# One layer of a hybrid attention / gated-linear-attention encoder: the product of probabilities and V in plain float32, two heads side by side in the column halves of the TensorE array

## The chip, the core and the metric

The kernel runs on one core of a Trainium2 chip. The metric is the device time of one execution in microseconds (us). Inputs and output are float32.

## What is computed

One layer: a LayerNorm of `x` (2048 frames x 1024), one input projection, two groups of heads, an output projection, a gated embedding and a second LayerNorm. The change lies in group A, chunked softmax attention with 8 heads of 64. Cut to what matters:

```python
h = layer_norm(x, ln_in_g, ln_in_b)
proj = h @ w_in                       # aq, ak, av, ag (512 each), then group B's parts
# per 64-frame chunk c and head: its own chunk and the 8 chunks before it
sc = einsum('bhqd,bhkd->bhqk', q_blk, k_blk) * scale + bias
sc = where(valid, sc, -1e30)
pr = softmax(sc, axis=-1)
att = einsum('bhqk,bhkd->bhqd', pr, v_blk)       # the product that is changed
att = att * silu(ag)
mix = concatenate([att, gla * silu(gg)]) @ w_out
```

Group B is gated linear attention with 4 heads. It is not touched, but some of its products have the form that the change brings in.

## The kernel before

The 2048 frames are two super-blocks `sb` of 1024, and each of these two groups `g` of 512 frames. For each super-block three phases follow each other: `gla_phase` (group B), `attn_phase` (group A) and `out_phase` (output projection, embedding, LayerNorm).

**Precision by halves.** The kernel gives most products to the array in a type `F32R`, rounded, which shows as one matmul record in the trace for each matmul of the program. To keep float32's accuracy it splits an operand into a rounded copy (`hi`) and the rest (`lo`) and adds the products: three matmuls (`hi*hi`, `hi*lo`, `lo*hi`) make one product of the projections (`gemm`, L317; V's own projection `gemm_v`, L917). A product of two plain `F32` operands shows as two records for each matmul.

**Attention.** `attn_phase` works on four pairs `pr` of heads. Each step of `attn` is one block of 128 queries of one head `h`: `pr`, `g`, then `h`, `qp` (which pair of query blocks) and `a` (which block of the pair). For a step
- `S` makes the scores, up to 5 key blocks of 128, with Q in halves (L993, L995); DVE adds the bias and takes the maximum (L999), ACT takes the exponential and the sum (L1003), and `norm` divides on POOL (L1011);
- `T` turns the probabilities block by block on TensorE (L1029, three blocks to a PSUM tile `PT`, of which there are two), and takes them out of PSUM twice: ACT writes the rounded copy `PTh` (L1031), DVE the rest `PTl` (L1032);
- `PV`, once for each head and pair of query blocks (64 calls), multiplies by V. Its weights are the 128 columns [hi of V | lo of V] of one head and key block, and its moving operand is 256 queries of `PTh`, then of `PTl`: 12 matmuls for a full call of 6 key blocks, each 128 columns wide (L1049). The first and the last of a call's key blocks concern only 128 of the queries. So the 128 partitions of the result `PV` hold 64 rows of products with V's hi and 64 with its lo;
- `fold`, for each head and group (32 times), adds these two: ACT copies one half of the partitions (L1062), DVE adds the other (L1063). After the second head DVE multiplies by the SiLU gate (L1065).

`ev_v` splits V into hi and lo as it leaves PSUM (ACT L932, DVE L933) and stores to DRAM (`vhist`) what a later step needs; `v_load` and `hist` fetch it.

**What sets the order.** Attention's steps run beside the projections as a side generator: `gemm` calls `tick()` every 4 matmuls, and the generator is advanced by as much as its due times say. The framework's scheduler then orders each engine's queue.

Of the kernel before, what the change touches and what calls it, by code (L numbers as in the profile page):

```python
# [26 lines left out]
F32 = mybir.dt.float32  # L27
F32R = mybir.dt.float32r
I32 = mybir.dt.int32
AF = mybir.ActivationFunctionType  # L30
OP = mybir.AluOpType
# [13 lines left out]
def hymba_layer_kernel(  # L45
# [15 lines left out]
    nc = tc.nc  # L61
    seq = x.shape[0]
    NSB = seq // 1024
# [6 lines left out]
    pool_t = ctx.enter_context(tc.tile_pool(name="pool_t", bufs=4))  # L70
    small = ctx.enter_context(tc.tile_pool(name="small", bufs=4))
    dram = ctx.enter_context(tc.tile_pool(name="dram", bufs=1, space=bass.MemoryType.DRAM))
# [3 lines left out]
    def U(name, dt=F32):  # L76
        return pool_u.tile([128, 512], dt, name=name, tag="u")
# [50 lines left out]
    mix = [[None, None] for _ in range(8)]  # L128
# [356 lines left out]
    def silu_evac(ps, k, g, first):  # L485
        t = U("t")
        nc.scalar.activation(t, ps, AF.Tanh, scale=0.5)
        if first:
            mix[k][g] = U("mix")
            nc.vector.scalar_tensor_tensor(mix[k][g], t, 1.0, ps, op0=OP.add, op1=OP.mult)  # L490
        else:
            nc.vector.scalar_tensor_tensor(t, t, 1.0, ps, op0=OP.add, op1=OP.mult)
            nc.vector.scalar_tensor_tensor(mix[k][g], t, 0.5, mix[k][g], op0=OP.mult, op1=OP.mult)
# [1 line left out]

    Fd = dram.tile([8, 64, 768], F32, name="relrows")
    khist = dram.tile([4, 2, 128, 512], F32, name="khist")
    vhist = dram.tile([2, 4, 2, 2, 128, 512], F32, name="vhist")

    def rel_load():  # L500
        ext = pool_t.tile([128, 6, 256], F32, name="ext", tag="t").rearrange("p a b -> p (a b)")[0:8, 0:768]
# [368 lines left out]
    def attn_phase(sb):  # L870
        es = ExitStack()
        aps = None
        Q = {}
        K = {}
        V = {}
# [49 lines left out]
                w_done(i + 1)  # L925

        def ev_v(ps, pr, g, bp):
            p5 = ps.rearrange("p (b e h d) -> p b e h d", b=2, e=2, h=2)
            for e in range(2):
                t = U("v", F32R)  # L930
                t4 = t.rearrange("p (b h d) -> p b h d", b=2, h=2)
                nc.scalar.activation(t4[:, :, :, 0:64], p5[:, :, e], AF.Copy)  # L932
                nc.vector.tensor_tensor(t4[:, :, :, 64:128], p5[:, :, e],  # L933
                                        t4[:, :, :, 0:64].bitcast(F32), op=OP.subtract)
                if e == 0:
                    V[pr, g, bp] = t
                if e or g and sb + 1 < NSB:
                    nc.sync.dma_start(vhist[sb % 2, pr + e, g, bp], t.bitcast(F32))

        def v_load(pr, g, bp):  # L940
            V[pr, g, bp] = t = U("v", F32R)
            nc.sync.dma_start(t.bitcast(F32), vhist[(sb if g >= 0 else sb - 1) % 2, pr, g % 2, bp])

        def hist(pr, h):
            if sb == 0:
                return
            K[pr, -1, h] = t = U("k", F32R)
            nc.sync.dma_start(t.bitcast(F32), khist[pr, h])
            v_load(pr, -1, h)

        bias = {}

        def load_bias(pr, h):
            f = Fd[:]
            bias[pr, h] = t = pool_p.tile([128, 640], F32, name="bias", tag="p")
            nc.gpsimd.memset(t[64:128, 0:64], NEG)
            nc.gpsimd.memset(t[0:64, 576:640], NEG)
            with tc.issue_after(queued[-1]):
                for r0 in (0, 64):
                    nc.sync.dma_start(t[r0:r0 + 64, r0:r0 + 576], bass.AP(  # L960
                        tensor=f.tensor, offset=f.offset + (2 * pr + h) * 64 * 768 + 127,
                        ap=[[767, 64], [1, 576]]))

        steps = [(pr, g, h, qp, a) for pr in range(4) for g in range(2) for h in range(2)
                 for qp in range(2) for a in range(2)]
        st = {}
        pts = {}
        pvs = {}
        att = {}

        def blk(n):
            pr, g, h, qp, a = steps[n]
            i = sb * 8 + g * 4 + 2 * qp + a
            return i, min(i, 4) + 1
# [32 lines left out]
        def norm(n):  # L1007
            ncol = blk(n)[1] * 128
            P, s4 = st[n]
            nc.vector.reciprocal(s4[:, 3:4], s4[:, 2:3])  # L1010
            nc.gpsimd.tensor_scalar(P[:, :ncol], P[:, :ncol], s4[:, 3:4], 1.0,  # L1011
                                    op0=OP.mult, op1=OP.mult)

        def T(n):
            a = steps[n][4]
            i, nkb = blk(n)
            P, _ = st.pop(n)
            if a == 0:
                pts[n // 2] = (pool_t.tile([128, 6, 256], F32R, name="PTh", tag="t"),
                               pool_t.tile([128, 6, 256], F32R, name="PTl", tag="t"))  # L1020
            Th, Tl = pts[n // 2]
            k0 = max(0, i - a - 4)
            d = i - nkb + 1 - k0
            cs = slice(a * 128, (a + 1) * 128)
            for b0 in range(0, nkb, 3):
                nb = min(3, nkb - b0)
                ps = aps.tile([128, 3, 128], F32, name="PT", bufs=2)
                for b in range(nb):
                    nc.tensor.transpose(ps[:, b, :], P[:, (b0 + b) * 128:(b0 + b + 1) * 128], ident)  # L1029
                ks = slice(d + b0, d + b0 + nb)  # L1030
                nc.scalar.activation(Th[:, ks, cs], ps[:, :nb, :], AF.Copy)  # L1031
                nc.vector.tensor_tensor(Tl[:, ks, cs], ps[:, :nb, :], Th[:, ks, cs].bitcast(F32),  # L1032
                                        op=OP.subtract)

        def PV(n):
            pr, g, h, qp, _ = steps[n]
            i, _ = blk(n - 1)
            Th, Tl = pts.pop(n // 2)
            if qp == 0:
                pvs[pr, g, h] = aps.tile([128, 512], F32, name="PV")  # L1040
            pv = pvs[pr, g, h]
            k0 = max(0, i - 4)
            ks = [i] + [b for b in range(k0, i + 2) if b != i]
            jobs = [(T_, b) for T_ in (Th, Tl) for b in ks]
            for m, (T_, b) in enumerate(jobs):
                c0 = 128 if b == i + 1 else 0
                c1 = 128 if b == i - 4 else 256
                gi, kb = b // 4 - 2 * sb, b % 4
                nc.tensor.matmul(pv[:, qp * 256 + c0:qp * 256 + c1],  # L1049
                                 lhsT=V[pr, gi, kb // 2][:, kb % 2 * 256 + h * 128:kb % 2 * 256 + h * 128 + 128],  # L1050
                                 rhs=T_[:, b - k0, c0:c1], start=(m == 0),
                                 stop=(m == len(jobs) - 1))
            if qp == 1:
                fold(pr, g, h)

        def fold(pr, g, h):
            pv = pvs.pop((pr, g, h))
            if h == 0:
                att[pr, g] = U("pvt")
            t = att[pr, g]  # L1060
            r, o = slice(64 * h, 64 * h + 64), slice(64 - 64 * h, 128 - 64 * h)
            nc.scalar.activation(t[r, :], pv[o, :], AF.Copy)  # L1062
            nc.vector.tensor_tensor(t[r, :], pv[r, :], t[r, :], op=OP.add)  # L1063
            if h == 1:
                nc.vector.scalar_tensor_tensor(mix[pr][g], t, 0.5, mix[pr][g],  # L1065
                                               op0=OP.mult, op1=OP.mult)
                del att[pr, g]

        def attn():
            N = len(steps)  # L1070
            for n in range(N + 4):
                if 0 <= n - 1 < N:
                    norm(n - 1)
                if n < N:
                    pr, g, h, qp, a = steps[n]
                    if pr % 2 and n % 8 < 2:
                        v_load(pr, g, n % 8)
                    if g == 1 and qp == 1 and a == 1 and pr < 3:
                        S(n)
                        load_bias(pr + 1, h)  # L1080
                        hist(pr + 1, h)
                    else:
                        S(n)
                yield
                if n >= 4 and steps[n - 4][4] == 1:
                    PV(n - 4)
                if 0 <= n - 2 < N:
                    T(n - 2)
                yield 2

        run = attn()

        def gate(i, pr, g):
            gemm(i, 8, 0, h_rhs(g), lambda ps: silu_evac(ps, pr, g, True), g == 1)

        for pr in range(4):
            odd = pr % 2
            idx = take(4)
            for g in range(2):
# [20 lines left out]
                if aps is None:  # L1120
                    edge.pop("close")()
                    aps = es.enter_context(tc.tile_pool(name="attnps", bufs=1, space=bass.MemoryType.PSUM))
        gg = take(2)
        set_side(run, scale=0.7, delay=1)
        for g in range(2):
            for n in range(2):
                gemm(gg[n], 8, 0, h_rhs(g),
                     lambda ps, n=n, g=g: silu_evac(ps, 6 + n, g, False), g == 1)
# [227 lines left out]
```

## Time and profile before

| | |
|---|---|
| time, three runs | 1384.40, 1390.73, 1391.21 us, median 1390.73 |
| the profiled execution's own time | 1383.77 us |
| its span in the trace | 1381.9 us |
| granted TensorE clock, mean | 0.993 |
| busy: TensorE matmuls, weight loads | 97%, 84% of the span |
| busy: DVE, ACT, POOL | 60%, 44%, 11% |

The profiled execution is 0.5% below the median of the runs and next to the lowest of them. A matmul record's end is modelled, and records overlap each other; how long a run of matmuls really holds the engine is read from the starts: from the first record's start to the start of what follows.

### The profile page before, as it was taken

The page shows a single profiled execution, that of the slowest core. Times are in us where ns is not written, and L with a number is a line of the kernel's source. Part 1 is how long each engine was busy: PE and PEld are TensorE (multiplying, and loading weights), DVE is VectorE, ACT ScalarE, POOL GpSimd, SP SyncE. Part 2 cuts the span into 40 slices and gives each one's busy share as a digit, 9 for nine tenths or more (in the row PEclk, how much of TensorE's full clock was granted, in tenths as well). Part 3 has the DMA queues.
Part 4 walks back from the last instruction along what each step waited for, and adds up shares of the span by engine and source line. Part 5 has one row for each costly group of instructions (what it writes and reads, how often), then busy time and mean ns, then how long its engine had stood idle before and what let it go on. Part 6 is the DMA issues. An engine that isn't in the chain of part 4 may idle for free.

```text
span 1381.9 us, 22143 instructions
## 1 busy us (share of the span) xinstructions
PE 1339.8 (97%) x8440; PEld 1166.5 (84%) x8440; DVE 829.1 (60%) x1833; ACT 609.7 (44%) x1200; POOL 154.0 (11%) x233
## 2 busy tenths in 40 slices
PE   5999999999999999999999999999999999999995
PEld 5889888889888888888898988988998888888875
DVE  7765636766576955546884552566566667332286
ACT  4755525555555722624544542455544555112222
POOL 1000101111111100000100100111211120000012
PEclk9999999999999999999999999999999999999998
DMA  8361516332533335766622132322232213335551
GB/s 323 57 192 48 200 62 229 107 140 71 191 117 130 130 122 197 272 224 229 202 77 108 62 109 80 135 94 90 82 107 101 85 47 111 111 108 196 203 187 61
DMA packets 63441, 186.39 MB, mean 135 GB/s; under 512 B 7216, under 2 KB 9320, under 8 KB 63336
## 3 DMA queue, kind: packets, MB, share of 16 engines
q1 hardware_dynamic: 62816, 183.41, 37.6%
q10 hardware_dynamic: 520, 1.57, 1.1%
q8 instruction: 67, 1.10, 0.3%
q14 instruction: 38, 0.31, 0.1%
HBM read 119.28 MB, written 65.67 MB: 134 GB/s over the span
## 4 chain that ended last, share of the span: by engine, by line
PE 81%; DVE 8%; ACT 5%; issue 2%; DMA 2%; POOL 1%; SPq 0%; ACTq 0%; DVEq 0%; POOLq 0%
PE proj L317 51%; PE proj L917 7%; PE proj L557 4%; PE PV L1049 4%; PE PT L1029 4%; PE S L995 2%; PE S L993 2%; DMA wraw<-in_wi_dram 1%; PE O L704 1%; DVE P L999 1%; ACT P L1003 1%; DVE PTl L1032 1%; ACT whi L286 1%; DVE wlo L291 1%; ACT qh L885 1%
## 5 line engine op out<-in xcount | busy, mean ns | idle before, releaser
L317 PE MATMUL proj<-hh,whi 128*128 128x512 f32 (+1 forms) x912 | 358.8, 393 | 2.3 <-DVE ql L888 0.8
L317 PE MATMUL proj<-hh,wlo 128*128 128x512 f32 (+1 forms) x912 | 357.4, 392 | 0.0
L317 PE MATMUL proj<-hl,whi 128*128 128x512 f32 (+1 forms) x912 | 354.2, 388 | 0.0
L317 PEld LDWEIGHTS proj<-hh,whi 128*128 128x128 f32 x912 | 172.9, 190 | 31.6 <-issue 1.0
L317 PEld LDWEIGHTS proj<-hl,whi 128*128 128x128 f32 x912 | 172.6, 189 | 29.1
L317 PEld LDWEIGHTS proj<-hh,wlo 128*128 128x128 f32 x912 | 172.5, 189 | 29.1
L1003 ACT ACTIVATE P<-P,s 128x640 f32<-128x640 f32 (+4 forms) x128 | 97.5, 762 | 154.7 <-DVE s L1002 134.5
L1011 POOL TENSOR_SCALAR P<-P,s 128x640 f32<-128x640 f32 (+4 forms) x128 | 95.9, 749 | 505.1 <-DVE s L1010 379.4
L999 DVE CUSTOM_DVE_ANT_0 P<-S,bias 128x640 f32<-128x640 f32 (+4 forms) x128 | 94.5, 738 | 48.8 <-PE S L995 42.8
L1032 DVE TENSOR_TENSOR PTl<-PT,PTh 128x384 fp32r<-128x384 f32 (+2 forms) x232 | 102.6, 473 | 14.9 <-ACT PTh L1031 13.1
L317 PE MATMUL proj<-mh,whi 128*128 128x512 f32 x256 | 99.9, 390 | 0.0
L317 PE MATMUL proj<-mh,wlo 128*128 128x512 f32 x256 | 99.8, 390 | 0.0
L159 POOL TENSOR_TENSOR rstd<-v,nhalf 128x1 f32<-128x1 f32 (+2 forms) x44 | 33.2, 761 | 570.9 <-DVE v L157 522.0
L1031 ACT ACTIVATE PTh<-PT 128x384 fp32r<-128x384 f32 (+2 forms) x232 | 87.0, 420 | 20.1 <-PE PT L1029 18.9
L1029 PE MATMUL PT<-ident,P 128*128 128x128 f32 x560 | 84.5, 275 | 1.0 <-DVE PTl L1032 0.8
L291 DVE TENSOR_TENSOR wlo<-wraw,whi 128x1024 fp32r<-128x1024 f32 (+1 forms) x46 | 56.1, 1225 | 46.6 <-ACT whi L286 44.8
L317 PE MATMUL proj<-ml,whi 128*128 128x512 f32 x192 | 75.2, 392 | 0.0
L917 PE MATMUL proj<-whi,hh 128*128 128x256 f32 x256 | 74.5, 291 | 0.0
L557 PE MATMUL proj<-whi,hl 128*128 128x272 f32 (+1 forms) x256 | 74.0, 293 | 0.0
L557 PE MATMUL proj<-whi,hh 128*128 128x272 f32 (+1 forms) x256 | 73.2, 293 | 0.7 <-ACT glr L574 0.7
L917 PE MATMUL proj<-wlo,hh 128*128 128x256 f32 x256 | 72.5, 283 | 0.0
L917 PE MATMUL proj<-whi,hl 128*128 128x256 f32 x256 | 72.4, 283 | 0.0
(221 smaller groups left out, 2512.8 us busy)
## 6 DMA issues: line engine op xcount, KB each, us to landing
whi<-wkept SPq DMA_DIRECT2D x64, 512.0 KB, 3.6
wlo<-wkept SPq DMA_DIRECT2D x64, 512.0 KB, 4.5
wkept<-whi SPq DMA_DIRECT2D x44, 512.0 KB, 2.9
wkept<-wlo SPq DMA_DIRECT2D x44, 512.0 KB, 3.5
wraw<-in_wi_dram SPq DMA_DIRECT2D x26, 512.0 KB, 5.5
x<-in_x_dram SPq DMA_DIRECT2D x32, 256.0 KB, 5.4
out_dram<-ysb SPq DMA_DIRECT2D x32, 256.0 KB, 2.1
v<-vhist SPq DMA_DIRECT2D x24, 256.0 KB, 3.6
```

The source lines that it names most:

```text
L159: nc.gpsimd.tensor_tensor(r[:, :n], v1[:, :n], nhalf[:, :n], op=OP.pow)
L291: nc.vector.tensor_tensor(lo, raw, hi.bitcast(F32), op=OP.subtract)
L317: nc.tensor.matmul(ps[:, cols], lhsT=l[:, c0 + k, :], rhs=rhs(k)[m][:, cols], start=(j == 0), stop=(j == n - 1))
L557: nc.tensor.matmul(ps[:, c0:c0 + nw], lhsT=h[k][g][:, b * 128:(b + 1) * 128], rhs=W[k // 4][m][:, k % 4, :], start=(n == 0), stop=(n == 23))
L917: nc.tensor.matmul(ps[:, bb * 256:bb * 256 + 256], lhsT=h[k][g][:, c], rhs=W[k // 4][m][:, k % 4, :], start=(k == 0 and n == 0), stop=(k = ...
L999: nc.vector.tensor_tensor_reduce(P[:, :ncol], ps[:, 512 - n_prev:512 + n_cur], bias[pr, h][:, 640 - ncol:640], 1.0, -3e38, OP.add, OP.max, ...
L1003: nc.scalar.activation(P[:, :ncol], P[:, :ncol], AF.Exp, bias=s4[:, 1:2], scale=1.0, accum_out=s4[:, 2:3])
L1011: nc.gpsimd.tensor_scalar(P[:, :ncol], P[:, :ncol], s4[:, 3:4], 1.0, op0=OP.mult, op1=OP.mult)
L1029: nc.tensor.transpose(ps[:, b, :], P[:, (b0 + b) * 128:(b0 + b + 1) * 128], ident)
L1031: nc.scalar.activation(Th[:, ks, cs], ps[:, :nb, :], AF.Copy)
L1032: nc.vector.tensor_tensor(Tl[:, ks, cs], ps[:, :nb, :], Th[:, ks, cs].bitcast(F32), op=OP.subtract)
L1049: nc.tensor.matmul(pv[:, qp * 256 + c0:qp * 256 + c1], lhsT=V[pr, gi, kb // 2][:, kb % 2 * 256 + h * 128:kb % 2 * 256 + h * 128 + 128], rh ...
```

## The change

Neither V nor the probabilities are split any more. V is stored once, in float32, for both heads of a pair: a tile of four key blocks by 128 columns, head 0 in columns 0 to 63 and head 1 in 64 to 127. The steps are ordered `qp` before `h`, so the two heads of a pair of query blocks are ready together, and `PV` is called once for both (32 calls). For each key block it issues two float32 matmuls with 64 weight columns each, head 0 into partitions 0 to 63 of the result and head 1 into 64 to 127. The result then holds both heads as the output projection wants them: `fold` is gone, and DVE multiplies by the gate straight from PSUM. `T` takes each `PT` tile out once: the first three blocks by ACT, the others by DVE.

```diff
-    vhist = dram.tile([2, 4, 2, 2, 128, 512], F32, name="vhist")
+    vhist = dram.tile([2, 4, 2, 128, 512], F32, name="vhist")
...
         def ev_v(ps, pr, g, bp):
...
-                t = U("v", F32R)
...
-                nc.scalar.activation(t4[:, :, :, 0:64], p5[:, :, e], AF.Copy)
-                nc.vector.tensor_tensor(t4[:, :, :, 64:128], p5[:, :, e],
-                                        t4[:, :, :, 0:64].bitcast(F32), op=OP.subtract)
...
+                t = V[pr + e, g]
+                nc.scalar.activation(t.rearrange("p (b c) -> p b c", c=128)[:, 2 * bp:2 * bp + 2, :],
+                                     p4[:, :, e], AF.Copy)
...
-        steps = [(pr, g, h, qp, a) for pr in range(4) for g in range(2) for h in range(2)
-                 for qp in range(2) for a in range(2)]
+        steps = [(pr, g, h, qp, a) for pr in range(4) for g in range(2) for qp in range(2)
+                 for h in range(2) for a in range(2)]
...
-                nc.scalar.activation(Th[:, ks, cs], ps[:, :nb, :], AF.Copy)
-                nc.vector.tensor_tensor(Tl[:, ks, cs], ps[:, :nb, :], Th[:, ks, cs].bitcast(F32),
-                                        op=OP.subtract)
+                if b0:
+                    nc.vector.tensor_copy(pt[:, ks, cs], ps[:, :nb, :])
+                else:
+                    nc.scalar.activation(pt[:, ks, cs], ps[:, :nb, :], AF.Copy)
...
-            jobs = [(T_, b) for T_ in (Th, Tl) for b in ks]
-            for m, (T_, b) in enumerate(jobs):
+            for m, b in enumerate(ks):
...
-                nc.tensor.matmul(pv[:, qp * 256 + c0:qp * 256 + c1],
-                                 lhsT=V[pr, gi, kb // 2][:, kb % 2 * 256 + h * 128:kb % 2 * 256 + h * 128 + 128],
-                                 rhs=T_[:, b - k0, c0:c1], start=(m == 0),
-                                 stop=(m == len(jobs) - 1))
+                for h in range(2):
+                    r = slice(64 * h, 64 * h + 64)
+                    nc.tensor.matmul(pv[r, qp * 256 + c0:qp * 256 + c1],
+                                     lhsT=V[pr, gi][:, kb * 128 + 64 * h:kb * 128 + 64 * h + 64],
+                                     rhs=pt[h][:, b - k0, c0:c1], start=(m == 0), stop=(m == len(ks) - 1))
             if qp == 1:
-                fold(pr, g, h)
-
-        def fold(pr, g, h):
...
-            nc.scalar.activation(t[r, :], pv[o, :], AF.Copy)
-            nc.vector.tensor_tensor(t[r, :], pv[r, :], t[r, :], op=OP.add)
-            if h == 1:
-                nc.vector.scalar_tensor_tensor(mix[pr][g], t, 0.5, mix[pr][g],
+                nc.vector.scalar_tensor_tensor(mix[pr][g], pvs.pop((pr, g)), 0.5, mix[pr][g],
                                                op0=OP.mult, op1=OP.mult)
...
-                if n >= 4 and steps[n - 4][4] == 1:
+                if n >= 4 and n % 4 == 3:
                     PV(n - 4)
```

The order on TensorE around one full call of `PV`, first before (a full call for one head; the call for the other head stands elsewhere and reads the same; `proj` is a projection's result, `x3` three such rows in a row):

```order
L317 MATMUL proj<-hh,wlo 128x512
L1049 MATMUL PV<-PTh,v 128x256
L1049 MATMUL PV<-PTh,v 128x128
L1049 MATMUL PV<-PTh,v 128x256 x3
L1049 MATMUL PV<-PTh,v 128x128
L1049 MATMUL PV<-PTl,v 128x256
L1049 MATMUL PV<-PTl,v 128x128
L1049 MATMUL PV<-PTl,v 128x256 x3
L1049 MATMUL PV<-PTl,v 128x128
L1029 MATMUL PT<-ident,P 128x128 x2
L317 MATMUL proj<-hh,whi 128x512
```

and now (the call for both heads, which alternate row by row; 64 is the number of result rows, so of weight columns):

```order
L917 MATMUL proj<-wlo,hh 128x256
L1050 MATMUL PV<-PT,v 64x256 x2
L1050 MATMUL PV<-PT,v 64x128 x2
L1050 MATMUL PV<-PT,v 64x256 x6
L1050 MATMUL PV<-PT,v 64x128 x2
L1027 MATMUL PT<-ident,P 128x128 x2
L917 MATMUL proj<-whi,hh 128x256
```

Twice 12 rows of 128 columns in two places have become 12 float32 rows of 64 columns in one. No other matmul has come between them, in any of the 32 calls.

On DVE, around the end of a head's group (`PTl`, `pvt` and `mix` as above, `ISA P,s` is L999's bias and maximum, `wlo` a weight's low half), before:

```order
L1032 TENSOR_TENSOR PTl<-PT,PTh 128x2x128
L291 TENSOR_TENSOR wlo<-wraw,whi 128x1024
L1010 RECIPROCAL s_4291<-s_4291 128x1
L999 ISA P,s_4331<-S,bias 128x640
L999 ISA s_4331 128x1
L490 SCALAR_TENSOR_TENSOR mix<-t,proj 128x512
L1002 TENSOR_SCALAR s_4331<-s_4331 128x1
L1010 RECIPROCAL s_4331<-s_4331 128x1
L1063 TENSOR_TENSOR pvt<-PV,pvt 64x512
L1032 TENSOR_TENSOR PTl<-PT,PTh 128x3x128
L1065 SCALAR_TENSOR_TENSOR mix<-pvt,mix 128x512
L1032 TENSOR_TENSOR PTl<-PT,PTh 128x2x128
```

and now:

```order
L1030 COPY PT<-PT 128x2x128
L1001 TENSOR_SCALAR s_4063<-s_4063 128x1
L291 TENSOR_TENSOR wlo<-wraw,whi 128x1024
L1009 RECIPROCAL s_4063<-s_4063 128x1
L998 ISA P,s_4100<-S,bias 128x640
L998 ISA s_4100 128x1
L490 SCALAR_TENSOR_TENSOR mix<-t,proj 128x512
L1001 TENSOR_SCALAR s_4100<-s_4100 128x1
L1054 SCALAR_TENSOR_TENSOR mix<-PV,mix 128x512
L1030 COPY PT<-PT 128x2x128
```

The fold's add and the subtractions for blocks of three have gone from DVE's queue; one copy of at most two blocks is left for each step, and the gate's product reads PSUM. On DVE 232 subtractions `PTl` become 104 copies, on ACT 232 copies `PTh` become 128, and the 32 folds (one row on ACT, one on DVE) and DVE's 32 subtractions for V are gone.

## Rows read from the trace of the kernel before

**Rows 1.** The page: busy time by engine, TensorE and its clock in 40 slices.
```profile
PE 1339.8 (97%) x8440; PEld 1166.5 (84%) x8440; DVE 829.1 (60%) x1833; ACT 609.7 (44%) x1200; POOL 154.0 (11%) x233
...
PE   5999999999999999999999999999999999999995
...
PEclk9999999999999999999999999999999999999998
```
**Rows 2.** Windows with the attention; columns: length, busy us by engine (instructions), clock, DMA.
```profile
205.00:485.00 280.00, 277.25 (x1668) 243.00 (x1667) 194.92 (x491) 157.12 (x352) 46.35 (x76) 1.00 0.39 138
845.00:1160.00 315.00, 314.28 (x1958) 280.10 (x1958) 198.87 (x498) 159.32 (x359) 53.06 (x76) 1.00 0.28 94
```
**Rows 3.** Waits of TensorE: who waited for whom, us in total, times, longest.
```profile
PE S L993 <- ACT qh L885: 1.1, 4, 0.4
PE PT L1029 <- DVE PTl L1032: 0.8, 2, 0.4
PE proj L317 <- DVE ql L888: 0.8, 1, 0.8
...
PE proj L317 <- DVE k L901: 0.3, 1, 0.3
```
**Rows 4.** TensorE in order of time around one full call: start, length, count.
```profile
391.60 0.39 PE L317 MATMUL proj<-hh,whi 128*128 128x512 f32 x1
391.83 0.81 PE L1049 MATMUL PV<-PTh,v 128*128 128x256 f32 x6
392.48 0.86 PE L1049 MATMUL PV<-PTl,v 128*128 128x256 f32 x6
393.18 0.73 PE L1029 MATMUL PT<-ident,P 128*128 128x128 f32 x5
```
**Rows 5.** Groups by line and shape, TensorE: xcount | busy us, mean ns of one.
```profile
L1049 PE MATMUL PV<-PTl,v 128*128 128x256 f32 x224 | 45.8, 308 | 0.0
L1049 PE MATMUL PV<-PTh,v 128*128 128x256 f32 x224 | 42.2, 292 | 0.0
...
L1049 PE MATMUL PV<-PTl,v 128*128 128x128 f32 x112 | 25.1, 224 | 0.0
...
L1049 PE MATMUL PV<-PTh,v 128*128 128x128 f32 x112 | 24.9, 222 | 0.0
...
L657 PE MATMUL kvp<-gv,kdT 128*64 128x128 f32 x128 | 8.8, 279 | 0.0
```
**Rows 6.** Order of time: group B's float32 product with 64 weight columns, two heads.
```profile
69.29 0.39 PE L317 MATMUL proj<-hl,whi 128*128 128x512 f32 x1
69.52 0.39 PE L317 MATMUL proj<-hh,wlo 128*128 128x512 f32 x1
69.84 1.09 PE L657 MATMUL kvp<-gv,kdT 128*64 128x128 f32 x16
70.86 0.50 PE L317 MATMUL proj<-hh,whi 128*128 128x512 f32 x1
71.20 0.40 PE L317 MATMUL proj<-hl,whi 128*128 128x512 f32 x1
```
**Rows 7.** Order of time: group B's float32 product with 128 weight columns.
```profile
79.88 2.05 PE L704 MATMUL O<-gv,att 128*128 128x128 f32 x16
81.68 0.47 PE L317 MATMUL proj<-hh,whi 128*128 128x512 f32 x1
```
**Rows 8.** Groups of weight loads: xcount | busy us, mean ns of one.
```profile
L1049 PEld LDWEIGHTS PV<-PTh,v 128*128 128x128 f32 x336 | 47.5, 189 | 4.3
...
L657 PEld LDWEIGHTS kvp<-gv,kdT 128*64 128x64 f32 x128 | 6.8, 136 | 1.9 <-issue 1.1 <-ACT kdT L647 0.4
```
**Rows 9.** Order of time: group B's 64 by 64 products, starts of two rounds.
```profile
73.70 0.39 PE L679 MATMUL CN<-qf,kn 64*64 64x64 f32 x9
...
74.05 0.39 PE L679 MATMUL CN<-qf,kn 64*64 64x64 f32 x9
```
**Rows 10.** Groups of DVE and of ACT that the change touches.
```profile
L1032 DVE TENSOR_TENSOR PTl<-PT,PTh 128x384 fp32r<-128x384 f32 (+2 forms) x232 | 102.6, 473 | 14.9 <-ACT PTh L1031 13.1
...
L1063 DVE TENSOR_TENSOR pvt<-PV,pvt 64x512 f32<-64x512 f32 x32 | 22.0, 689 | 12.3 <-ACT pvt L1062 12.2
L933 DVE TENSOR_TENSOR v<-proj,v 128x256 fp32r<-128x256 f32 x32 | 13.6, 424 | 18.9 <-ACT v L932 17.8
...
L1031 ACT ACTIVATE PTh<-PT 128x384 fp32r<-128x384 f32 (+2 forms) x232 | 87.0, 420 | 20.1 <-PE PT L1029 18.9
...
L1062 ACT ACTIVATE pvt<-PV 64x512 f32<-64x512 f32 x32 | 18.9, 592 | 2.2 <-PE PV L1049 0.8 <-ACT P L1003 0.2
```

More of the change, by code (lines that the diff above doesn't have):

```diff
@@ L927, in ev_v, with v_load @@
         def ev_v(ps, pr, g, bp):
-            p5 = ps.rearrange("p (b e h d) -> p b e h d", b=2, e=2, h=2)
+            p4 = ps.rearrange("p (b e c) -> p b e c", b=2, e=2)
             for e in range(2):
-                t = U("v", F32R)
-                t4 = t.rearrange("p (b h d) -> p b h d", b=2, h=2)
-                nc.scalar.activation(t4[:, :, :, 0:64], p5[:, :, e], AF.Copy)
-                nc.vector.tensor_tensor(t4[:, :, :, 64:128], p5[:, :, e],
-                                        t4[:, :, :, 0:64].bitcast(F32), op=OP.subtract)
[L935 to L942, printed above, removed]
+                if bp == 0:
+                    V[pr + e, g] = U("v")
+                t = V[pr + e, g]
+                nc.scalar.activation(t.rearrange("p (b c) -> p b c", c=128)[:, 2 * bp:2 * bp + 2, :],
+                                     p4[:, :, e], AF.Copy)
+                if bp and (e or g and sb + 1 < NSB):
+                    nc.sync.dma_start(vhist[sb % 2, pr + e, g], t)
+        def v_load(pr, g):
+            V[pr, g] = t = U("v")
+            nc.sync.dma_start(t, vhist[(sb if g >= 0 else sb - 1) % 2, pr, g % 2])
         def hist(pr, h):
@@ L948, in hist @@
             nc.sync.dma_start(t.bitcast(F32), khist[pr, h])
-            v_load(pr, -1, h)
+            if h == 0:
+                v_load(pr, -1)
         bias = {}
@@ L1018, in T @@
             if a == 0:
-                pts[n // 2] = (pool_t.tile([128, 6, 256], F32R, name="PTh", tag="t"),
-                               pool_t.tile([128, 6, 256], F32R, name="PTl", tag="t"))
-            Th, Tl = pts[n // 2]
+                pts[n // 2] = pool_t.tile([128, 6, 256], F32, name="PT", tag="t")
+            pt = pts[n // 2]
             k0 = max(0, i - a - 4)
@@ L1030, in T @@
                 ks = slice(d + b0, d + b0 + nb)
-                nc.scalar.activation(Th[:, ks, cs], ps[:, :nb, :], AF.Copy)
-                nc.vector.tensor_tensor(Tl[:, ks, cs], ps[:, :nb, :], Th[:, ks, cs].bitcast(F32),
-                                        op=OP.subtract)
+                if b0:
+                    nc.vector.tensor_copy(pt[:, ks, cs], ps[:, :nb, :])
+                else:
+                    nc.scalar.activation(pt[:, ks, cs], ps[:, :nb, :], AF.Copy)
         def PV(n):
-            pr, g, h, qp, _ = steps[n]
+            pr, g, _, qp, _ = steps[n]
             i, _ = blk(n - 1)
-            Th, Tl = pts.pop(n // 2)
+            pt = pts.pop(n // 2 - 1), pts.pop(n // 2)
             if qp == 0:
-                pvs[pr, g, h] = aps.tile([128, 512], F32, name="PV")
-            pv = pvs[pr, g, h]
+                pvs[pr, g] = aps.tile([128, 512], F32, name="PV")
+            pv = pvs[pr, g]
             k0 = max(0, i - 4)
             ks = [i] + [b for b in range(k0, i + 2) if b != i]
-            jobs = [(T_, b) for T_ in (Th, Tl) for b in ks]
-            for m, (T_, b) in enumerate(jobs):
+            for m, b in enumerate(ks):
                 c0 = 128 if b == i + 1 else 0
@@ L1048, in PV @@
                 gi, kb = b // 4 - 2 * sb, b % 4
-                nc.tensor.matmul(pv[:, qp * 256 + c0:qp * 256 + c1],
-                                 lhsT=V[pr, gi, kb // 2][:, kb % 2 * 256 + h * 128:kb % 2 * 256 + h * 128 + 128],
-                                 rhs=T_[:, b - k0, c0:c1], start=(m == 0),
-                                 stop=(m == len(jobs) - 1))
-            if qp == 1:
-                fold(pr, g, h)
-        def fold(pr, g, h):
[L1057 to L1061, printed above, removed]
-            nc.scalar.activation(t[r, :], pv[o, :], AF.Copy)
-            nc.vector.tensor_tensor(t[r, :], pv[r, :], t[r, :], op=OP.add)
-            if h == 1:
-                nc.vector.scalar_tensor_tensor(mix[pr][g], t, 0.5, mix[pr][g],
+                for h in range(2):
[3 more added lines that the diff above has]
+                                     rhs=pt[h][:, b - k0, c0:c1], start=(m == 0), stop=(m == len(ks) - 1))
+            if qp == 1:
+                nc.vector.scalar_tensor_tensor(mix[pr][g], pvs.pop((pr, g)), 0.5, mix[pr][g],
                                                op0=OP.mult, op1=OP.mult)
-                del att[pr, g]
         def attn():
@@ L1075, in attn @@
                     pr, g, h, qp, a = steps[n]
-                    if pr % 2 and n % 8 < 2:
-                        v_load(pr, g, n % 8)
+                    if pr % 2 and n % 8 == 0:
+                        v_load(pr, g)
                     if g == 1 and qp == 1 and a == 1 and pr < 3:
```

## The prediction

> **What bounds the kernel now.** I read the page first. TensorE is busy in nine tenths or more of every slice but the first and the last, at a granted clock of nine tenths or more (the 2.4 GHz level), while DVE is busy 60% and ACT 44% [rows 1]. A busy TensorE proves little, since its records overlap, so the second view is the two windows that hold the attention: 277.25 of 280 us and 314.28 of 315 us busy, at clock 1.00 [rows 2]. The third is the list of TensorE's waits. In the attention it waited for another engine 1.1 + 0.8 + 0.8 + 0.3 = 3.0 us in all [rows 3]. So the attention stages take as long as TensorE's own queue takes, and whatever leaves DVE, ACT or the DMA queues can give back those 3.0 us and little more. The change is therefore a question of how long TensorE needs for the new form of the product.
>
> **TensorE, what goes.** A full call of PV for one head starts at 391.83 and the next work at 393.18: 1.35 us for 12 records, 112 ns each, though a third of them are only half as wide [rows 4]. There are 448 records of 256 columns and 224 of 128 [rows 5]. At 112 ns the 672 take 75.3 us. The turn from a projection into the call costs nothing that shows: 391.60 to 391.83 is 0.23 us, as from one projection matmul to the next [rows 4, 6].
>
> **TensorE, what comes.** 336 float32 matmuls of 64 weight columns. The program before has this very form in group B: L657, two heads in the two column halves, alternating, in float32. Its 64 matmuls in the program are 128 records in the trace [rows 5], two for each, so the new PV will have 672 records again: 448 of 256 columns, 224 of 128, half of them in each column half.
> - *Stream.* Sixteen L657 records start from 69.84 on and are all done 1.09 us later. A record takes 279 ns from start to modelled end, so the last starts 0.81 us after the first: 15 steps of 54 ns [rows 5, 6]. With 128 weight columns a float32 record of the same width takes (81.68 - 79.88) / 16 = 112 ns [rows 7]. So the two column halves work at the same time, and a pair of records, one in each half, takes 2 x 54 = 109 ns at 128 columns. No row has float32 at 256 columns. I take 2 x 109 = 218 ns a pair. The lower bound is 214 ns (twice the 107 that remain if about 2 ns of each are fixed; an estimate), the upper 231 ns (what 512 one-pass columns take, 69.29 to 69.52 [rows 6]). Sum: 224 pairs x 0.218 + 112 pairs x 0.109 = 48.8 + 12.2 = 61.0 us, between 60 and 64.
> - *Turns.* From 69.52 to 71.20 lie two projection records and the sixteen of L657 [rows 6]. Two projections at 0.23 are 0.46, eight pairs at 0.109 are 0.87; of the 1.68 us 0.35 remain. That is the price of going into the split array and back: the start after the first projection is 0.09 late (0.32 for 0.23), the first projection after it takes 0.34 for 0.23, the rest lies in between. 32 calls make 32 such visits: 11.2 us. Before, PV paid none. After the call transposes follow, not a projection, which no row shows; bounds 0.15 (only the way in) and 0.45 us a visit: 5 to 14 us.
>
> New total 61.0 + 11.2 = 72.2 against 75.3 us: **3.1 us saved**, with the bounds together from 10 saved to 3 lost. I keep the middle, as both prices come from the same form in the same program.
>
> **DVE and ACT.** DVE loses 102.6 us of subtractions, 22.0 of folds and 13.6 for V, and gains 104 copies of at most two blocks; at 0.42 us, what the subtraction of 256 columns for V takes, that is 44 us at most. ACT loses 18.9 us of folds and some 87.0 x 104 / 232 = 39 us of copies [rows 10]. None of it bounds anything: TensorE covers it. What it reaches are the waits of rows 3: a `PT` tile is now free after one copy of about 0.42 us and no longer after 0.42 on ACT and then 0.47 on DVE, and Q's and K's low halves come earlier in DVE's queue. I count 2 of the 3.0 us, between 0 and 3. What TensorE waits for next is ACT's Q copies, which stay.
>
> **What moves at no cost.** The step order: scores, transposes and their counts stay, and a call of PV comes two steps after its last transposes, so its operands have been copied long before. The last fold of a group (ACT 0.59, then DVE 0.69 us) leaves the chain to the output projection; TensorE had other blocks to multiply meanwhile (314.28 of 315 us busy [rows 2]), so I count nothing. V's history goes through DRAM in half as many transfers on SP's queue; no wait of TensorE in the attention names a DMA. If K's and the bias's transfers, issued two steps later for head 0, came late, a score matmul would wait; they have the rest of the pair's steps as cover.
>
> **Sum:** -3.1 - 2.0 = -5.1 us. Against the profiled execution's own 1383.8 us that is 1378.7; it is 7 us below the median of the runs, 1390.73, against which I give **1385.6 us**. A difference of 0.5%, 7 us, is about what a measurement of this kernel can tell from no change; this forecast lies under it.
>
> **The rivals.**
> - *The weights are not loaded ahead (slower).* If a column half could not take new weights while it works, every record would pay its load. 128 weight columns take 189 ns and 64 take 136 [rows 8], so 64 columns are worth 53 ns; 336 loads in each half, both halves at once, are 17.8 us: 1385.6 + 17.8 = 1403. It decides from about 15 ns exposed a record, where the 5 us are gone. Against it: L657 would need 53 ns on top of each 107, and its pairs follow at 109. It could be that 109 hides a 53 ns load and a 53 ns stream; but then the 64 by 64 products, six records to the busiest quarter of the array in 73.70 to 74.05, 58 ns each [rows 9], would need 53 + 27 = 80. The Trainium skill, "TensorE: Matmul & The Clock Gate", section on packing small matmuls, has a rule for this rival: a weight load overlaps running matmuls only where the row group differs, and here all four row groups are used by both halves. The trace does not agree: matmuls are busy 97% and loads 84% of the same span, nearly all with all rows. Chance 6%.
> - *The halves work one after the other at 256 columns (slower).* Then 448 x 0.218 + 224 x 0.109 = 122 us instead of 61: 1447 us. For it: no row has two halves at this width with sums that build up over six blocks. Against it: rows 6. Chance 3%.
> - *The visits cost half, and all waits go (faster).* With 0.15 us a visit 6 us more are saved, and with the 3.0 us of waits gone 1 more: 1378.5 us, or down to 1374 with all bounds. For it: the way back into transposes may be cheaper than into a projection, and smaller delays, under what the wait list names, sit between TensorE's records in the attention and go with a shorter DVE queue. Against it: the 0.34 us after L657 look like a drained array, whatever comes next. Chance 31%.
> - *The stream takes 231 ns, or visits 0.45 (nothing won, or a little lost).* 1389 to 1393 us. Part of the forecast's own range.
>
> **How the numbers follow.** The forecast (1385.6, its own range 1380 to 1393) has 60%, the faster rival 31%, the two slower 6% and 3%. The range 1373 to 1395 takes the forecast and the faster rival in and leaves the two slower ones out, with a little for the runs' own spread of 7 us. Faster by over 0.5%: the 31% and a part of the forecast's lower end, 0.37. Slower by over 0.5%: 0.09 for the two rivals and 0.01 from the upper end, 0.10. Within 0.5%: 0.53.
>
> **What would show it.** In the profile after: 672 records of PV with 64 columns, starting in pairs, pairs about 218 ns apart at 256 columns (right), 270 (weights exposed) or 430 (one after the other); a full call for both heads taking 12 pairs, 8 x 0.218 + 4 x 0.109 = 2.18 us, from its start to its last record's end in the array, against 2 x 1.35 = 2.70 before; a first projection or transpose after it late by 0.1 us or so; the clock at 1.00 in both attention windows; DVE's busy time lower by some 90 us, ACT's by some 60; TensorE's waits in the attention under 2 us. I am wrong if the pairs are not pairs, or if TensorE begins to wait for something not on the list above.

## The result: 0.990 of the time before, and the profile after

The changed kernel took 1371.76 us (median of 4 runs, 1370.4 to 1373.85) against 1387.57 us for the kernel before, measured beside it. The ratio on record is 0.9898, with a 95% interval of 0.9876 to 0.9919: 14 us or 1% faster (the medians alone lie 15.8 us apart). Two later comparisons on other occasions gave 0.9899 (0.988 to 0.9918) and 0.9901 (0.9879 to 0.9922). I had forecast 0.4% and called that no difference; the measured median lies 1.2 us under the low end of my range. Applied to the 1390.73 us that I forecast against, the ratio gives 1376.5 us, inside the range and 9 us under the forecast.

The page of the changed kernel, busy time by engine and TensorE's clock, answers to [rows 1]:

```profile
PE 1332.9 (97%) x8440; PEld 1132.1 (83%) x8440; DVE 739.2 (54%) x1641; ACT 562.1 (41%) x1064; POOL 154.1 (11%) x233
...
PEclk9999999999999999999999999999999999999998
```

The number of TensorE records is the same, DVE lost 89.9 us, as forecast, and ACT 47.6 us, where some 60 were forecast: the 128 copies that stay on it are the long ones (464 ns, where all 232 had a mean of 420). TensorE's busy share says nothing, as before.

Where did the time go? I cut both traces at TensorE's own marks: from the first score matmul to the start of the last PV record, in each super-block. Columns of the windows view: length, then busy us of TensorE, weight loads, DVE, ACT, POOL, then the granted clock and the DMA. The kernel before:

```profile
202.75:473.98 271.23, 268.41 (x1624) 235.35 (x1623) 185.55 (x480) 150.95 (x341) 46.35 (x76) 1.00 0.38 133
856.79:1154.68 297.89, 297.17 (x1865) 265.13 (x1863) 191.99 (x487) 152.94 (x348) 53.06 (x76) 1.00 0.27 92
```

The changed kernel:

```profile
204.37:468.66 264.29, 264.16 (x1625) 219.97 (x1623) 146.17 (x390) 133.19 (x288) 45.09 (x76) 1.00 0.36 128
851.81:1143.61 291.80, 291.76 (x1864) 244.29 (x1863) 148.78 (x398) 126.94 (x270) 54.46 (x76) 1.00 0.25 85
```

The attention stages take 569.1 us before and 556.1 us after: **13.0 us**, 6.9 in the first super-block and 6.1 in the second. Between them and after them nothing moved by more than 0.4 us. Only the head, before the first score matmul, differs at random: 202.75 us in the profile before, 204.37 in this one, 203.38 and 207.92 in two more profiles of the same changed kernel, up to 209.5 in the others below. The 569.1 us come from the one profile of the kernel before. So I compare attention stages of profiles, and times only with their intervals.

TensorE in order of time around one full call, after (start, length, count), answers to [rows 4]:

```profile
395.77 0.39 PE L317 MATMUL proj<-hl,whi 128*128 128x512 f32 x1
395.99 0.39 PE L317 MATMUL proj<-hh,wlo 128*128 128x512 f32 x1
396.31 2.39 PE L1050 MATMUL PV<-PT,v 128*64 128x256 f32 x24
398.63 0.77 PE L1027 MATMUL PT<-ident,P 128*128 128x128 f32 x5
399.15 0.47 PE L317 MATMUL proj<-hh,whi 128*128 128x512 f32 x1
```

and its groups by shape, which answer to [rows 5]:

```profile
L1050 PE MATMUL PV<-PT,v 128*64 128x256 f32 x448 | 59.5, 386 | 0.0
...
L1050 PE MATMUL PV<-PT,v 128*64 128x128 f32 x224 | 21.7, 273 | 0.0
```

Both heads' full call now takes 396.31 to 398.63, 2.32 us, where the old form took two times 1.35 us [rows 4]. Its last record starts 2.39 - 0.27 = 2.12 us after the first. That is eight pairs of 256 columns, three of 128 at 0.109 us and about 0.05 us for the first, so about 217 ns a pair (six pairs of 256 columns that follow each other from 397.01 to 398.31 are 216 ns apart): the halves run side by side, the second pass of each record included, as group B's did at half the width. The visit shows at three places: 395.99 to 396.31 is 0.32 us where 0.23 is usual (0.09); the call's 2.32 us exceed its 8 x 0.217 + 4 x 0.109 = 2.17 by 0.15; the five transposes after it take 0.52 us where 0.46 is usual after a projection (0.06). Together 0.30 us.

TensorE's waits in the attention, [rows 3], are all gone from the list of the changed kernel; DVE's and ACT's evacuations, which answer to [rows 10], are now:

```profile
L1030 DVE COPY PT<-PT 128x256 f32<-128x256 f32 (+1 forms) x104 | 42.8, 411 | 24.1 <-PE PT L1027 22.5
```

```profile
L1032 ACT ACTIVATE PT<-PT 128x384 f32<-128x384 f32 (+2 forms) x128 | 59.3, 464 | 50.8 <-PE PT L1027 50.1
```

From the starts, TensorE's own share of the 13.0 us can be worked out. The 32 calls take 65.4 us from their starts to what follows (24 of 2.32, four of 1.67, four of 0.80), the 64 calls before took 74.9. Of the 9.5 us the ways in and the slower transposes give back 3.5 (32 x 0.09, 32 x 0.06, less 64 x 0.02 that the transposes had after the old form): **6.0 us from the form**. Some 7 us are something else.

### The profile page after: what moved, and what is told of

It is laid out like the page before. It is cut to its first block, busy times and chain, and to the rows that moved or that the text cites. A ratio compares the mean times of both kernels' runs of the same rounds, so it can differ in the third digit from the quotient of the medians.

```text
span 1371.0 us, 21628 instructions
## 1 busy us (share of the span) xinstructions
PE 1332.9 (97%) x8440; PEld 1132.1 (83%) x8440; DVE 739.2 (54%) x1641; ACT 562.1 (41%) x1064; POOL 154.1 (11%) x233
## 4 chain that ended last, share of the span: by engine, by line
PE 89%; DVE 5%; ACT 3%; DMA 1%; issue 1%; POOL 0%; SPq 0%; ACTq 0%; DVEq 0%; POOLq 0%
PE proj L317 56%; PE proj L917 7%; PE PT L1027 5%; PE PV L1050 5%; PE proj L557 5%; PE S L994 3%; PE S L992 2%; PE O L704 1%; DMA wraw<-in_wi_dram 1%; PE kvp L657 1%; PE O L700 1%; DVE ysb L397 1%; PE CN L679 1%; PE CN L317 0%; DVE ysb L399 0%
## 5 line engine op out<-in xcount | busy, mean ns | idle before, releaser
L1032 ACT ACTIVATE PT<-PT 128x384 f32<-128x384 f32 (+2 forms) x128 | 59.3, 464 | 50.8 <-PE PT L1027 50.1
L1027 PEld LDWEIGHTS PT<-ident,P 128*128 128x128 f32 x560 | 65.3, 140 | 14.2 <-issue 5.1
L888 DVE SCALAR_TENSOR_TENSOR ql<-proj,qh 64x512 fp32r<-64x512 f32 x64 | 44.0, 688 | 53.2 <-ACT qh L885 51.5
```

The lines of the kernel that those rows point to most:

```text
L888: nc.vector.scalar_tensor_tensor(ql[h][o, :], ps[r, :], QSCALE, qh[h][r, :].bitcast(F32), op0=OP.mult, op1=OP.subtract)
L1032: nc.scalar.activation(pt[:, ks, cs], ps[:, :nb, :], AF.Copy)
```

## The experiments

Theory A: 6 us come from TensorE's form, 7 from waits for ACT and DVE. Theory B: the form gives it all and the lighter evacuation nothing. Four kernels ran beside each other first.

**The change once more.**

> The changed kernel as it is, on the chip of the runs beside it, so that they can be compared with it. Both theories: 0.990 of the time before (0.987 to 0.993).

0.9899 (0.988 to 0.9918). Its attention stages take 264.83 + 291.81 = 556.6 us, so a repeated profile agrees within 0.6 us.

**The evacuation work put back.** Edit, cut (the fold and V's subtraction were put back in the same manner):

```diff
-                if b0:
-                    nc.vector.tensor_copy(pt[:, ks, cs], ps[:, :nb, :])
-                else:
-                    nc.scalar.activation(pt[:, ks, cs], ps[:, :nb, :], AF.Copy)
+                nc.scalar.activation(pt[:, ks, cs], ps[:, :nb, :], AF.Copy)
+                low = U("low", F32R).rearrange("p (b q) -> p b q", q=128)[:, :nb, :]
+                nc.vector.tensor_tensor(low, ps[:, :nb, :], pt[:, ks, cs], op=OP.subtract)
```

> The changed kernel with the work on ACT and DVE that the change took away put back beside it, its results unused: the subtraction after each copy out of a PT tile, the fold's copy and add for each head, V's subtraction. TensorE's work is that of the changed kernel. Theory A (of some 13 us that the attention stages gained between the two profiles, about 6 are TensorE's shorter form and about 7 are waits for ACT and DVE that went): most of the 7 us come back, 0.995 of the time before (0.993 to 0.998). Theory B (the new form on TensorE gives all of it, the lighter ACT and DVE nothing): as the changed kernel, 0.990.

0.9928 (0.9909 to 0.9948), 1376.51 us. The page shows that the work is back, 824.5 and 610.6 us on DVE and ACT:

```profile
PE 1337.1 (97%) x8440; PEld 1134.2 (82%) x8440; DVE 824.5 (60%) x1833; ACT 610.6 (44%) x1200; POOL 154.4 (11%) x233
```

Its attention stages:

```profile
206.64:473.19 266.55, 265.73 (x1624) 220.39 (x1623) 183.53 (x479) 150.07 (x339) 46.44 (x76) 1.00 0.37 127
856.12:1149.53 293.41, 292.89 (x1865) 244.17 (x1863) 188.41 (x485) 152.28 (x345) 53.38 (x76) 1.00 0.25 85
```

560.0 us: 3.3 to 3.9 us of the 13 come back. Neither theory's number: B is out, and A has only half of its 7 us. About 3 us were open.

Not all of it is a wait. The matmuls are those of the changed kernel, but the scheduler has placed some of them otherwise, and one call is cut in two, its first two records apart from the other 22:

```profile
1097.95 0.65 PE L1053 MATMUL PV<-PT,v 128*64 128x256 f32 x2
1098.53 0.50 PE L317 MATMUL proj<-hh,whi 128*128 128x512 f32 x1
...
1105.72 2.38 PE L1053 MATMUL PV<-PT,v 128*64 128x256 f32 x22
1108.03 0.44 PE L1031 MATMUL PT<-ident,P 128*128 128x128 f32 x2
```

Its two parts hold TensorE 0.58 + 2.31 us where the whole call takes 2.32; with the second way in and out that is some 0.8 us. So the evacuation itself accounts for about 2.5 to 3.1 us in this run.

**Sixteen visits in place of 32.** Edit, cut (the tile of turned probabilities has five slots, the pool five tiles):

```diff
-                if n >= 4 and n % 4 == 3:
-                    PV(n - 4)
+                if n >= 4 and n % 8 == 3:
+                    PV(n - 8)
+                    PV(n - 4)
```

> The changed kernel with the calls for both pairs of query blocks of a group issued together: 16 visits to the split array in place of 32, the same matmuls. For room a tile of turned probabilities has five slots in place of six (the first and the last key block share one) and there are five tiles in place of four. Theory A (a visit costs about 0.28 us on TensorE beyond its matmuls): 16 x 0.28 = 4.5 us less than the changed kernel, 0.987 of the time before. Rival C (turning the array costs nothing; what shows at its edges is in the modelled times alone): as the changed kernel, 0.990.

0.9902 (0.9879 to 0.9926): in the times no gain. **64 visits.** Edit: `PV(n, part)` issues the first half of the key blocks at `n % 4 == 3`, the second one step later.

> The changed kernel with each call cut in two, the second half of the key blocks one step later, with projections and turns of the next step between: 64 visits in place of 32, the same matmuls. Theory A (0.28 us a visit): 9 us more than the changed kernel, 0.9965 of the time before. Rival C (turning costs nothing): as the changed kernel, 0.990.

0.9973 (0.9957 to 0.999), 1381.59 us. The attention stages of the two, first 16 and then 64 visits:

```profile
203.01:466.71 263.70, 262.95 (x1625) 220.73 (x1623) 148.25 (x393) 132.17 (x289) 45.09 (x76) 1.00 0.37 132
850.03:1140.15 290.12, 289.92 (x1864) 244.98 (x1863) 149.78 (x400) 126.08 (x272) 54.61 (x76) 1.00 0.26 89
```

```profile
209.09:478.02 268.93, 268.78 (x1625) 217.64 (x1623) 145.78 (x390) 132.98 (x288) 45.19 (x76) 1.00 0.35 126
861.56:1157.80 296.24, 296.20 (x1865) 241.94 (x1863) 148.99 (x398) 127.96 (x270) 54.35 (x76) 1.00 0.25 84
```

With twice the visits the stages take 565.2 us, 8.5 to 9.1 more than with 32: for 30 visits more (two of the 32 calls stayed whole in TensorE's order) 0.28 to 0.30 us each. The price of a visit is real, and rival C falls. With half the visits they take 553.8 us, 2.3 to 2.8 less where 4.7 were to be had. TensorE is busy 262.95 of 263.70 us in the first stage: a part of the gain turned into waits. Call a start late when it follows the start before it by over 0.1 us more than the median for the same neighbours in other places. By that measure 1.7 us are late in six places of these two stages, at a projection after transposes and at score matmuls, and none in the changed kernel's: that is most of what is missing.

Three more kernels went after the open 3 us, and after what the halves need.

**The light evacuation on the old form.** Edit, cut (no low halves of V, no fold, in the same manner):

```diff
-                pts[n // 2] = (pool_t.tile([128, 6, 256], F32R, name="PTh", tag="t"),
-                               pool_t.tile([128, 6, 256], F32R, name="PTl", tag="t"))
+                pts[n // 2] = (pool_t.tile([128, 6, 256], F32R, name="PTh", tag="t"),) * 2
...
-                nc.scalar.activation(Th[:, ks, cs], ps[:, :nb, :], AF.Copy)
-                nc.vector.tensor_tensor(Tl[:, ks, cs], ps[:, :nb, :], Th[:, ks, cs].bitcast(F32),
-                                        op=OP.subtract)
+                if b0:
+                    nc.vector.tensor_copy(Th[:, ks, cs], ps[:, :nb, :])
+                else:
+                    nc.scalar.activation(Th[:, ks, cs], ps[:, :nb, :], AF.Copy)
```

> The kernel before with TensorE's queue as it was, each matmul of PV with its old form and count, but ACT and DVE as light as in the change: each PT tile taken out once (three blocks by ACT, the others by DVE), no low halves of the probabilities and of V, no fold; the gate's product reads one head's result. It leaves out the low halves (the rounded copies stand in for them) and head 0's result. Theory A (the lighter evacuation alone takes waits away, some 4 us by the run with the evacuation put back): 0.997 of the time before (0.995 to 0.999). Rival D (waits go only where the calls for two heads are one and the steps come in the new order): 1.000.

0.9978 (0.9964 to 0.9992), 1382.82 us: 3 us faster by the lighter evacuation alone. Rival D falls. The kernel ran once more for its trace:

> The old form with the light evacuation once more, for its trace: where the 3 us that its times showed come from. It leaves out the low halves of the probabilities and of V and head 0's result. Theory A: TensorE's records of PV take 75 us as before, and the attention stages (from the first score matmul to the last of PV, both super-blocks) are some 3 us shorter than the 569 us before, with the waits for PTl gone. Rival D: 569 us, waits as before.

```profile
209.50:477.59 268.09, 266.84 (x1625) 236.00 (x1623) 145.10 (x389) 134.01 (x298) 46.10 (x76) 1.00 0.38 135
860.52:1157.67 297.15, 296.79 (x1865) 265.22 (x1863) 147.87 (x396) 129.77 (x281) 53.26 (x76) 1.00 0.28 92
```

565.2 us against 569.1, 3.9 us less, while the calls of PV take the same 74.9 us from their starts to what follows. By the measure above its starts are late by 2.8 us, against 5.6 in the kernel before. On the old form the lighter evacuation is worth 3.9 us by the stages and 3 by the times, on the new one about 2.5 to 3.1: some 3 to 4 us.

**The old step order on the new form.** Edit:

```diff
-        steps = [(pr, g, h, qp, a) for pr in range(4) for g in range(2) for qp in range(2)
-                 for h in range(2) for a in range(2)]
+        steps = [(pr, g, h, qp, a) for pr in range(4) for g in range(2) for h in range(2)
+                 for qp in range(2) for a in range(2)]
...
-            pt = pts.pop(n // 2 - 1), pts.pop(n // 2)
+            pt = pts.pop(n // 2 - 2), pts.pop(n // 2)
...
-                if n >= 4 and n % 4 == 3:
+                if n >= 8 and n % 8 in (1, 3):
```

> The changed kernel with the steps in the order of before (head, then pair of query blocks), so that the two calls of PV of a group come at its end, two steps apart, and no longer evenly; same matmuls, same 32 visits, same light evacuation. Theory D (the even order with one call for two heads gives the 3 us that neither the form nor the lighter evacuation accounts for): 3 us more than the changed kernel, 0.992 of the time before. Rival (order gives nothing): as the changed kernel, 0.990.

0.9924 (0.9905 to 0.9943), 1374.85 us. The interval takes in 0.992 and just leaves 0.990 out, but it overlaps the changed kernel's own (0.988 to 0.9918); the stages speak for the first theory:

```profile
202.86:468.62 265.76, 265.35 (x1624) 219.80 (x1623) 146.49 (x389) 131.36 (x288) 46.27 (x76) 1.00 0.36 128
851.65:1144.37 292.72, 292.52 (x1865) 244.27 (x1863) 149.18 (x398) 125.75 (x270) 54.19 (x76) 1.00 0.25 85
```

558.5 us, 1.8 to 2.4 more than the changed kernel, which repeats within 0.6. The even order gives about 2 us. So 6.0 (form) + 3 to 4 (evacuation) + 2 (order) make 11 to 12 of the 12.5 to 13.0 us; about one is left without a name. The late starts say the same: 5.6 us in the kernel before, none in the first profile of the changed kernel (0.5 in one of its repeats), 1.7 with the old order. With the form's 6.0 that is 11.6.

**The halves in turn.** Edit: the loop over the two heads outside the loop over the key blocks, nothing else.

> The changed kernel with the same matmuls in each call, but all key blocks of head 0 first and then all of head 1, so that rows that stand next to each other use the same column half. Theory A (the halves gain because a row of one half runs while a row of the other does): the 61 us of stream become nearly 122, less what overlaps where the heads meet: some 55 us more than the changed kernel, 1.030 of the time before (1.025 to 1.035). Rival E (a row of 64 columns is short by itself, whatever stands beside it): as the changed kernel, 0.990.

1.0197 (1.0176 to 1.0218), 1413.38 us: 41 us slower than the change. Rival E falls: a row of 64 columns is not short by itself, it gains by the neighbour in the other half. But it is 14 us better than I expected. One full call in its trace:

```profile
405.79 3.95 PE L1050 MATMUL PV<-PT,v 128*64 128x256 f32 x24
409.67 0.55 PE L1027 MATMUL PT<-ident,P 128*128 128x128 f32 x3
```

3.88 us, not the 4.48 that 24 records one after the other and the edges would take. The records of its line up to the start of head 1's first one (first and last start, forms):

```profile
L1050 PE MATMUL PV<-PT,v x9: 272/379/430, 405.8 to 407.4; 128*64 128x256 f32 x7, 128*64 128x128 f32 x2
```

and those from there on, of which two had started before:

```profile
L1050 PE MATMUL PV<-PT,v x17: 272/379/431, 407.1 to 409.5; 128*64 128x256 f32 x11, 128*64 128x128 f32 x6
```

Of head 0's twelve records nine had started; then head 1's first, which stands behind all twelve in the program, started at 407.36, beside the ninth. The first record of a half is known by its length, 430 ns where others of 256 columns take 379, and there is one in each of the two lists. Three of head 0 still waited. So a half does take work from behind rows that wait for the other half, but not from far behind.

**Blocks of three.** Edit: three key blocks of one head, then three of the other.

> The changed kernel with the rows of a call in runs of three key blocks for one head, then three for the other. A float32 matmul is two records, so six records of one half stand in a row. Theory F (from the run with the halves in turn, where head 1's first record began while three records of head 0 had not yet started: a half takes work from at most about three records past the oldest that waits): a full call takes 2.6 us and not 2.16 us from first start to last end of stream, so 24 full calls cost 10 us more than the changed kernel, 1382 us against 1372. Rival (the halves overlap completely as long as both have work in the same call): as the changed kernel; second rival (no overlap but where the heads meet): nearer to the run with the halves in turn, 1400 and more.

One run, 1390.91 us; its head was 4.5 us longer than the changed kernel's, so the stage and the calls decide. A full call:

```profile
404.40 2.87 PE L1051 MATMUL PV<-PT,v 128*64 128x256 f32 x24
407.20 0.76 PE L1027 MATMUL PT<-ident,P 128*128 128x128 f32 x5
```

2.80 us to the next start, of which 0.15 are the edges: 2.65 us, where theory F said 2.6, complete overlap 2.17 and none 4.3. The attention stages:

```profile
208.88:479.13 270.25, 270.06 (x1624) 226.36 (x1623) 146.83 (x390) 133.59 (x288) 45.11 (x76) 1.00 0.36 126
862.26:1161.66 299.40, 299.36 (x1864) 252.81 (x1863) 149.77 (x398) 127.04 (x270) 54.45 (x76) 1.00 0.25 84
```

They take 569.7 us, as long as before the change and 13.6 more than the changed kernel: 11.6 by the 24 full calls, where theory F said 10, and 1.9 by the four calls of four key blocks (2.15 us each, 1.67 in the changed kernel), which it had left out. The order of rows inside a call alone gives or takes the 13 us.

**Sixteen visits again**, beside the change.

> Sixteen visits once more, against the changed kernel on the same chip. In the trace of the first run its attention stages were 2.8 us shorter than the changed kernel's. Theory A: 2 to 3 us less than the run beside it, 0.988 of the time before. Rival: no difference that the times can show, 0.990.

> The changed kernel beside the run with sixteen visits, 0.990 of the time before in both theories.

0.9892 (0.9873 to 0.9911) and 0.9901 (0.9879 to 0.9922). The stages take 264.40 + 290.13 = 554.5 us and 264.25 + 291.77 = 556.0 us: 1.5 us less, and 2.5 us of late starts in eight places. The times can't show it, so no version is shown to beat the changed kernel.

## Why the prediction was half right

- **TensorE bounds the attention: right.** The gain lies in the attention stages alone, and DVE's 90 and ACT's 48 us of saved work became 3 to 4 us.
- **The stream: right.** 218 ns a pair was forecast, 216 to 217 came; 12 pairs in 2.17 us, forecast 2.18. Neither slower rival came true: the weights are loaded ahead and the halves overlap. That also settles the rule of the Trainium skill that I weighed against it ("TensorE: Matmul & The Clock Gate", section on packing small matmuls): taken by itself it would put pairs at an estimated 270 ns (217 and the 53 of a load); they follow at 217, so it does not hold here.
- **The step that failed first, "turns" (0.35 us a visit, 11.2 us):** 0.30 measured from the edges, 0.28 to 0.30 from the run with 64 visits. That is 1.6 us of the error. Another 0.9 is on the old form's side, which held TensorE for 74.9 us and delayed the transposes behind it by 1.3, where I had 75.3 and nothing; 0.4 is the stream. So the form gave 6.0 us and not 3.1. The mechanism was right, the size off by 3 us.
- **The step that failed most, "I count 2 of the 3.0 us, between 0 and 3":** the bound was wrong. I took the wait list for the whole. That list counts the time between one record's modelled end and the next start. In the kernel before the transposes at 371.94 were followed by a projection at 373.20, which the list has as a wait of 0.77 us:

```profile
371.94 0.49 PE L1029 MATMUL PT<-ident,P 128*128 128x128 f32 x3
373.20 0.47 PE L317 MATMUL proj<-hh,whi 128*128 128x512 f32 x1 [0.77 <-DVE ql L888]
```

  Three transposes and a turn to a projection elsewhere take 0.25 us and not 1.26: 1.0 us lost. Against the same neighbours elsewhere, the starts in the attention are late by 5.6 us in 13 places, each by over 0.1 us. All of it went, the waits for ACT's Q copies too, which I had expected to stay. The lighter evacuation alone gave 3 to 4 us.
- **"The step order ... at no cost":** about 2 us gained. I had looked only for a loss there.
- **The faster rival (31%)** had the time, 1378.5 us or down to 1374, by cheaper visits and by waits beyond the list. Its second half is what the runs show; visits at half price are not. The time scaled to the runs before, 1376.5 us, lies under the forecast's own 1380 to 1393 and in the range only because the range took this rival in; the sum had 5.1 us where the stages gained 13.0, with both of its terms too small.

## What to carry to other kernels

Two products with 64 weight columns each cost no more than one with 128 if the two halves of the array alternate row by row (109 ns against 112 for records of 128 columns [rows 6, 7]); put three blocks of one half in a row and 13 of 569 us are gone again. Count the visits to a split array (0.3 us each here) and keep each one whole. Where one engine bounds a stage, bound what lighter neighbours can give by the lateness of its starts against the same neighbours elsewhere, not by the list of its waits.

## What I had not expected of the hardware

TensorE started matmul records out of the program's order when they belong to different column halves (that the queue kept the program's order inside a call is taken from the other calls, not seen in this one): head 1's first record ran beside head 0's ninth while three of head 0's had not started. Worked out from the starts, with that reach of three records and 216 and 109 ns a record, a full call takes 3.68 us with the halves in turn and 2.60 us in blocks of three; measured, without 0.15 us of edges, 3.73 and 2.65. The calls of four key blocks fit as well: 2.38 and 1.95 worked out, 2.43 and 2.00 measured. How the reach comes about, and whether it is the same for other widths of records, was not tried.
